# Placing a side stream of weight tiles in a two-block network kernel: where its loads, dots and transposes stand

## The chip, the cores and the metric

One core of a Trainium2 chip runs the whole program in one launch. The metric is device time in microseconds (us). The engines are TensorE (PE, with its weight loads shown apart as PEld), VectorE (DVE), ScalarE (ACT), GpSimd (POOL) and SyncE (SP), which issues nearly all transfers.

## What is computed

256 tokens of width 1024 go through two blocks. The first block has two layers; each has a SwiGLU feed-forward, a token mixer (convolution, state space, attention) and a second feed-forward. Ahead of each of these, and in its residual sum, stand shifts, scales and gates that come from a vector `c` through a large matrix `ada_w`:

```python
for l in range(DEPTH):
    mod = (jax.nn.silu(c) @ ada_w[l] + ada_b[l]).reshape(bsz, 3, 3, 1, D_MODEL)
    u = modulate(h, mod[:, 0, 0], mod[:, 0, 1])            # h * (1 + scale) + shift
    y = swiglu_ffn(u, ffn_w_gate[l, 0], ffn_w_up[l, 0], ffn_w_down[l, 0])
    h = layer_norm(DN_ALPHA * h + MACARON_WEIGHT * mod[:, 0, 2] * y, ln_g[l, 0], ln_b[l, 0])
    u = modulate(h, mod[:, 1, 0], mod[:, 1, 1])
    y = hybrid_token_mixer(u, ...)
    h = layer_norm(DN_ALPHA * h + mod[:, 1, 2] * y, ln_g[l, 1], ln_b[l, 1])
    u = modulate(h, mod[:, 2, 0], mod[:, 2, 1])
    y = swiglu_ffn(u, ffn_w_gate[l, 1], ffn_w_up[l, 1], ffn_w_down[l, 1])
    h = layer_norm(DN_ALPHA * h + MACARON_WEIGHT * mod[:, 2, 2] * y, ln_g[l, 2], ln_b[l, 2])
```

The second block (two more layers with a mixer and a feed-forward) takes no such values.

## The kernel before

**Sections and units.** The program is a list of sections that follow each other: FFN00, mixer0, FFN01 (layer 0), FFN10, mixer1, FFN11 (layer 1), then the second block. A section is a list of units. A unit is half a weight chunk: one transfer of 128 x 1024 f32 (512 KB) on SP into a ring of 4 buffers (`load_half`, L179), a split into a rounded high part on ACT (`hi`, L185) and a rest on DVE (`lo`, L186), and some 12 to 24 matmuls that use both (L282 to L284, L295 to L297). `run` traces the splits up to four units ahead of the matmuls. Between units, `step_sides` moves side work on at a given rate per unit: convolutions (`ca`, L1203), attention, state space, and the modulation stream.

**The modulation stream** (`ada_stream`). There are 18 columns (2 layers x 9) of 8 tiles each. A tile is one transfer of 512 KB (L489, ring of 3 buffers, `ada`) and one dot on DVE that multiplies it with `crow` and sums along the row (L490). The first 16 tiles are done by `First.start`; 128 are left for the stream. After the eighth tile of a column a bias is added (L503). Each third column (a gate) is also turned into a row: a PE transpose (L508), an ACT copy and a small store to `growd`, from which the closing norm of a section fetches it (`Ln.fetch`). `need` runs the stream on by force when a section wants values that are not there yet. `set_pace` sets the stream's rate: 26 tiles for each FFN and each mixer, spread over most of its units; `Ln.affine`, near a section's end, sets it to zero.

**What sets the order.** A scheduler of the tile framework orders the traced instructions of each engine, by its own estimates, within what dependencies allow. `behind(ins)` puts an edge without a semaphore: instructions traced inside it stand behind `ins` on that engine. An engine then runs its list strictly in order, and so does SP with its transfers: an instruction that waits holds all behind it.

**The close of a section.** `Ln.stats` (L606, L607) and `norm_T` (L430 and on) make the next section's operand from the accumulators `y`; PE has little else to do there.

Of the kernel before, what the change touches and what calls it, by code (L numbers as in the profile page):

```python
# [11 lines left out]
F32 = mybir.dt.float32  # L12
# [3 lines left out]
ALU = mybir.AluOpType  # L16
# [3 lines left out]
P = 128  # L20
T = 256
D = 1024
KT = 8
DEPTH = 2
# [81 lines left out]
def net_kernel(ctx, tc, a, out, dbg=None):  # L106
    nc = tc.nc
    V, S, G, E = nc.vector, nc.scalar, nc.gpsimd, nc.tensor

    const = ctx.enter_context(tc.tile_pool(name="const", bufs=1))  # L110
# [17 lines left out]
    def tp_tile():  # L128
        return p_tp.tile([P, 512], F32, tag="tp", name="tp")

    def rt(tag, n, bufs, dt=F32):
        return ring.tile([P, n], dt, tag=tag, name=tag, bufs=bufs)
# [4 lines left out]
    def f(ap):  # L137
        return ap.bitcast(F32)
# [13 lines left out]
    adb = const.tile([P, DEPTH, 72], F32, name="adb")  # L152
# [22 lines left out]
    def load_half(src, half, raw=None):  # L175
        n = max(D, src.shape[-1] // 2)
        if raw is None:
            raw = wraw.tile([P, DW], F32, tag="raw", name="raw")[:, :n]
        state["load"] = nc.sync.dma_start(raw, src[:, half * n:(half + 1) * n])  # L179
        return raw  # L180

    def split_half(src, half, c, room=None, eng=V):
        raw = load_half(src, half)
        hi, lo = room() if room else (wsp.tile([P, DW], F32R, tag=t, name=t)[:, :raw.shape[-1]] for t in ("hi", "lo"))
        S.activation(hi, raw, AF.Copy)  # L185
        eng.tensor_tensor(lo, raw, f(hi), op=ALU.subtract)  # L186
        return tuple(x.rearrange("p (k c) -> p k c", c=c) for x in (hi, lo))

    def split(u):
        u.w = split_half(u.ch.src, u.half, u.c, u.early or u.room)  # L190
# [6 lines left out]
    def set_early(items):  # L197
        units = [it for it in items if isinstance(it, Unit)][:4]
        for i, u in enumerate(units):
            u.early = lambda i=i: spare(i)  # L200
        return units
# [9 lines left out]
    def add_side(gen, rate, front=True):  # L211
        sides.insert(0 if front else len(sides), [gen, rate, 0.0])
        return gen
# [17 lines left out]
    state = {"live": 0}  # L231
# [17 lines left out]
    def behind(ins):  # L249

        es = ExitStack()
        for i in ins:
            es.enter_context(tc.issue_after(i.ins))
        return es
# [214 lines left out]
    mods, pcols = {}, {}  # L469
# [3 lines left out]
    def load_pcol(l):  # L473
        t = big.tile([P, NPC], F32, tag="pcol", name="pcol")
        late_load(t, a["pcol"][l])
        pcols[l] = t
# [7 lines left out]
            E.matmul(tp, ones[0:1, :P], crow[0:1, hs], start=True, stop=True)  # L484
            S.activation(crow[:, hs], tp, AF.Silu)

    def ada_tile(l, j, k, col, raw):
        n = D
        nc.sync.dma_start(raw, a["adaw"][l, j, k // 2][:, (k % 2) * n:(k % 2 + 1) * n])  # L489
        V.scalar_tensor_tensor(raw, raw, 1.0, crow, op0=ALU.mult, op1=ALU.mult, accum_out=col[:, k:k + 1])  # L490


    pace = {"after": ()}

    def ada_stream():
        for l, j in [(l, j) for l in range(DEPTH) for j in range(9)][2:]:
            col = const.tile([P, KT], F32, name="mod%d_%d" % (l, j))
            for k in range(KT):
                with behind(pace["after"]):
                    ada_tile(l, j, k, col, rt("ada", D, 3))  # L500
                pace["after"] = ()
                yield
            V.tensor_add(col, col, adb[:, l, j * 8:j * 8 + 8])  # L503
            mods[(l, j)] = col
            if j % 3 == 2:
                yield
                tp = tp_tile()
                E.transpose(tp[0:KT, :P], col, ident)  # L508
                gr = rt("t1", T, 4)[0:KT, :P]
                S.activation(gr, tp[0:KT, :P], AF.Copy, scale=(1.0 if j == 5 else 0.5))  # L510
                S.dma_start(growd[l * 3 + j // 3].rearrange("(k p) -> k p", p=P), gr)
                mods[(l, j, "row")] = True

    def set_pace(r, after=None):

        if "gen" not in pace:
            pace["gen"] = add_side(ada_stream(), 0.0, front=False)
        for s in sides:
            if s[0] is pace["gen"]:
                s[1] = r  # L520
        if after is not None:
            pace["after"] = after
# [236 lines left out]
    def ffn(cols, down, nj, src, act, rows, nxt):  # L759

        xT = lambda: src.xT
        y, hids, items = {}, {}, []

        def hidden(j):
            st = []

            def evac(ps):
                r = act(st, ps)
                if r is not None:
                    hids[j] = split_hidden(r)  # L770
            its = []
            for c in cols(j):
                its += proj_cols(c, xT, evac)
            return its
        hold = {"nx": nxt(y)}
        n0 = NFIRST if isinstance(src, First) else 2 // len(cols(0))
        done = 0
        for j in range(n0 - 1, nj):
            if j >= n0:
                items += hidden(j)  # L780
            elif isinstance(src, First):
                first = sum((cols(i) for i in range(n0)), [])
                items.append(lambda: src.start(first, rows, hids))
                continue
            else:
                items += first_hidden(sum((cols(i) for i in range(n0)), []), xT, rows, lambda: None, hids)
            if j == n0 + 1:
                items.append(src.residual)
            items += sum(down_items(y, hids, down, nj, range(done, j), hold), [])
            done = j  # L790
            per = 2 * len(cols(0)) + 2
            if j == nj - 1 - 32 // per:
                items.append(lambda: start_fetch(hold["nx"], 0.2))
            if j == nj - 1 - 24 // per:
                items.append(lambda: early(hold["nx"], 4, 0.25))
            if j == nj - 1:
                items.append(lambda: hold["nx"].prefetch())
        items += sum(down_items(y, hids, down, nj, [nj - 1], hold), [])
        return items, hold["nx"]
# [1072 lines left out]
    def ffn_section(cols, down, nj, act, rows, nxt, tiles):  # L1872
        src = cur
        items, nx = ffn(cols, down, nj, src, act, rows, nxt)
        src.pre += set_early(items)
        us = [i for i, it in enumerate(items) if isinstance(it, Unit)]
        rate = tiles / (len(us) - 18)
        if isinstance(src, First):
            items.insert(us[1], lambda: set_pace(rate, src.ins))
            items.insert(us[1], lambda: src.finish())  # L1880
        elif rate:
            items.insert(us[3], lambda: set_pace(rate, src.ins))
        return items, nx

    def mixer_section(fn, l, nxt, tiles=0.0):
        items, nx = fn(l, cur, nxt)
        src = cur
        src.pre += set_early(items)
        if tiles:
            units = [i for i, it in enumerate(items) if isinstance(it, Unit)]  # L1890
            rate = tiles / (len(units) - 16)
            items.insert(units[8], lambda: set_pace(rate, src.ins))
        return items, nx

    def close(nx):

        def start():
            nx.operand(0)
            state["after"] = nx.ins
            nx.operand(1)  # L1900
        return [lambda: nx.stats(1)] + ([start] if hasattr(nx, "operand") else [])

    for l in range(DEPTH):
        if l:
            prog.append(lambda l=l: load_pcol(l))
        for i in range(3):
            nxt = lambda y, l=l, i=i, src=cur: Ln(l, i, y, src)
            if i == 1:
                its, nx = mixer_section(mixer1, l, nxt, 26.0)
            else:  # L1910
                n = i // 2
                its, nx = ffn_section(lambda j: [a["wg"][l, n, j], a["wu"][l, n, j]], a["wd"][l, n], DFF // T, swiglu,
                                      swiglu_rows, nxt, 26.0)
            prog += its
            if not nx.last:
                prog += close(nx)
            cur = nx
# [56 lines left out]
    for l in range(DEPTH):  # L1974
# [5 lines left out]
        its, nx = mixer_section(mixer2, l, lambda y, l=l: Rms(y, lambda: qcols[l][:, QC_NF:QC_NF + 8]))  # L1980
        prog += its + close(nx)
        cur = nx
        if l + 1 < DEPTH:
            nxt = lambda y, l=l, src=cur: Rms(y, lambda: qcols[l + 1][:, QC_NM:QC_NM + 8], src)
        else:
            nxt = lambda y, src=cur: Out(y, src)
        its, nx = ffn_section(lambda j: [a["ff1"][l, j]], a["ff2"][l], DFF2 // T, relu2, lambda ps: relu2(None, ps), nxt, 0.0)
# [196 lines left out]
```

## Time and profile before

| | |
|---|---|
| median of three runs | 2521.87 us (2512.83 to 2522.38) |
| profiled execution | 2518.11 us |
| its span | 2516.3 us |
| mean granted TensorE clock | 0.987 of full speed |
| busy: PE / PEld / DVE / ACT | 95% / 87% / 73% / 54% |
| moved | 490 MB, mean 195 GB/s |

PE is busy nearly all the time, so what can be moved lies in the stretches where it is not, and in those where it is busy at the lower clock: a granted clock of 0.5 is 1.2 GHz, 1.0 is 2.4 GHz, and the same matmuls then count as more busy time. The sections are of few kinds, so the same code can be compared with and without the stream beside it. The section boundaries used below (213, 706, 926, 1122, 1582 and 1774 us) stand in the closes, within a few us of the first row of the next section's operand.

### The profile page before, as it was taken

The page shows a single profiled execution, that of the slowest core. Times are in us where ns is not written, and L with a number is a line of the kernel's source. Part 1 is how long each engine was busy: PE and PEld are TensorE (multiplying, and loading weights), DVE is VectorE, ACT ScalarE, POOL GpSimd, SP SyncE. Part 2 cuts the span into 40 slices and gives each one's busy share as a digit, 9 for nine tenths or more (in the row PEclk, how much of TensorE's full clock was granted, in tenths as well). Part 3 has the DMA queues.
Part 4 walks back from the last instruction along what each step waited for, and adds up shares of the span by engine and source line. Part 5 has one row for each costly group of instructions (what it writes and reads, how often), then busy time and mean ns, then how long its engine had stood idle before and what let it go on. Part 6 is the DMA issues. An engine that isn't in the chain of part 4 may idle for free. (4 is left out here: it accounts for less than half of the span.)

```text
span 2516.3 us, 42234 instructions
## 1 busy us (share of the span) xinstructions
PE 2401.0 (95%) x16444; PEld 2186.2 (87%) x16444; DVE 1838.0 (73%) x3262; ACT 1360.7 (54%) x2392; POOL 70.1 (3%) x128
## 2 busy tenths in 40 slices
PE   8999999999899979999999999999899999999999
PEld 6997889889789869988899898899789898799898
DVE  7789988899787677568988996655766555666544
ACT  5445677644544434455676555545465555565554
POOL 0000000000000000000000000000100000100000
PEclk9999999999999989999999999999999999999999
DMA  9897533356878867655433456467346566436464
GB/s 333 305 363 270 195 128 97 120 166 219 285 240 295 298 218 238 218 176 187 162 102 91 130 181 226 143 194 236 126 134 192 156 187 222 142 110 226 150 185 142
DMA packets 140058, 490.00 MB, mean 195 GB/s; under 512 B 16249, under 2 KB 21969, under 8 KB 139858
## 3 DMA queue, kind: packets, MB, share of 16 engines
q1 hardware_dynamic: 132194, 476.61, 57.3%
q10 hardware_dynamic: 7664, 10.69, 1.3%
q8 instruction: 129, 2.11, 0.3%
q14 instruction: 71, 0.58, 0.1%
HBM read 481.94 MB, written 5.31 MB: 194 GB/s over the span
## 5 line engine op out<-in xcount | busy, mean ns | idle before, releaser
L185 ACT ACTIVATE hi<-raw 128x1024 fp32r<-128x1024 f32 (+1 forms) x676 | 713.4, 1059 | 706.9 <-PE mm L283 386.4
L186 DVE TENSOR_TENSOR lo<-raw,hi 128x1024 fp32r<-128x1024 f32 (+1 forms) x676 | 825.0, 1223 | 313.5 <-ACT hi L185 311.4
L282 PE MATMUL mm<-xTh,hi 128*128 128x256 f32 x2896 | 826.8, 286 | 11.3 <-ACT seg L915 4.2
L284 PE MATMUL mm<-xTh,lo 128*128 128x256 f32 x2896 | 821.7, 284 | 3.9 <-DVE lo L186 3.9
L283 PE MATMUL mm<-xTl,hi 128*128 128x256 f32 x2896 | 821.7, 284 | 2.2 <-DVE xTl L453 2.2
L282 PEld LDWEIGHTS mm<-xTh,hi 128*128 128x128 f32 x2896 | 550.7, 190 | 16.7 <-ACT seg L915 4.3
L283 PEld LDWEIGHTS mm<-xTl,hi 128*128 128x128 f32 x2896 | 550.4, 190 | 6.5 <-DVE xTl L453 3.0
L284 PEld LDWEIGHTS mm<-xTh,lo 128*128 128x128 f32 x2896 | 550.3, 190 | 5.6 <-DVE lo L186 5.1
L297 PE MATMUL y<-hi,q 128*128 128x512 f32 x664 | 263.0, 397 | 0.3 <-DVE q L700 0.3
L296 PE MATMUL y<-lo,q 128*128 128x512 f32 x552 | 219.0, 397 | 6.6 <-DVE lo L186 6.5
L295 PE MATMUL y<-hi,q 128*128 128x512 f32 x552 | 219.5, 399 | 5.3 <-ACT q L699 5.2
L490 DVE SCALAR_TENSOR_TENSOR ada<-ada,crow 128x1024 f32<-128x1024 f32 x128 | 156.2, 1223 | 73.9 <-DMA ada<-in_adaw_dram 73.5
L1203 DVE SCALAR_TENSOR_TENSOR ca<-av,pcol,ca 128x226 f32<-128x226 f32 (+25 forms) x480 | 209.0, 468 | 0.3
L297 PEld LDWEIGHTS y<-hi,q 128*128 128x128 f32 x664 | 125.7, 189 | 31.1 <-DVE q L700 0.9
L296 PEld LDWEIGHTS y<-lo,q 128*128 128x128 f32 x552 | 104.0, 189 | 31.9 <-DVE lo L186 10.4
L295 PEld LDWEIGHTS y<-hi,q 128*128 128x128 f32 x552 | 104.0, 189 | 29.0 <-ACT q L699 7.2
L295 PE MATMUL y<-hi,xTh 128*128 128x512 f32 (+1 forms) x288 | 113.5, 394 | 2.8 <-DVE e8b L829 1.5
L283 PE MATMUL mm<-xyl,hi 128*128 128x256 f32 x384 | 109.9, 287 | 5.1 <-DVE xyl L413 5.1
L282 PE MATMUL mm<-xyh,hi 128*128 128x256 f32 x384 | 109.9, 287 | 3.3 <-ACT t2d L1371 3.0
L284 PE MATMUL mm<-xyh,lo 128*128 128x256 f32 x384 | 109.8, 286 | 3.1 <-DVE lo L186 3.1
L297 PE MATMUL y<-hi,xTl 128*128 128x512 f32 (+1 forms) x288 | 111.6, 388 | 0.0
L296 PE MATMUL y<-lo,xTh 128*128 128x512 f32 (+1 forms) x288 | 111.0, 385 | 0.0
(480 smaller groups left out, 3688.0 us busy)
## 6 DMA issues: line engine op xcount, KB each, us to landing
ada<-in_adaw_dram SPq DMA_DIRECT2D x128, 512.0 KB, 5.9
raw<-in_ff_dram SPq DMA_DIRECT2D x128, 512.0 KB, 4.5
raw<-in_wg_dram SPq DMA_DIRECT2D x88, 512.0 KB, 5.1
raw<-in_wu_dram SPq DMA_DIRECT2D x88, 512.0 KB, 4.7
raw<-in_wd_dram SPq DMA_DIRECT2D x88, 512.0 KB, 4.7
raw<-in_wG_dram SPq DMA_DIRECT2D x48, 512.0 KB, 3.8
raw<-in_wkv_dram SPq DMA_DIRECT2D x16, 512.0 KB, 4.4
raw<-in_wval_dram SPq DMA_DIRECT2D x16, 512.0 KB, 3.9
```

The costliest lines, as they stand in the source:

```text
L185: S.activation(hi, raw, AF.Copy)
L186: eng.tensor_tensor(lo, raw, f(hi), op=ALU.subtract)
L282: E.matmul(ps, wh[:, wk + k], xh, start=(k == 0), stop=False)
L283: E.matmul(ps, wh[:, wk + k], xl, start=False, stop=False)
L284: E.matmul(ps, wl[:, wk + k], xh, start=False, stop=(k == nk - 1))
L295: return [E.matmul(ps, xh, wh[:, kk, cs], start=first, stop=False), E.matmul(ps, xh, wl[:, kk, cs], start=False, stop=False), E.matmul(ps, ...
L296: E.matmul(ps, xh, wl[:, kk, cs], start=False, stop=False),
L297: E.matmul(ps, xl, wh[:, kk, cs], start=False, stop=last)]
L490: V.scalar_tensor_tensor(raw, raw, 1.0, crow, op0=ALU.mult, op1=ALU.mult, accum_out=col[:, k:k + 1])
L1203: V.scalar_tensor_tensor(ca[:, k, s:T], av[:, 0:T - s], caw[:, k, w:w + 1], ca[:, k, s:T], op0=ALU.mult, op1=ALU.add)
```

## The change

The load and the dot of a tile become separate functions. The stream is written as steps. Step n traces the load of tile n, placed behind the newest weight load on SP; then, if one is due, the transpose of a gate's column that was completed three steps before; then the dot of tile n-1, placed behind the newest `lo` on DVE. So a dot is traced one step later than its load. No tile, transpose or bias is added or dropped.

The rates change too: FFN00 38 tiles, FFN01 31, FFN10 31, FFN11 16 (all spread over 9 units more than before), and 11 in each mixer, between its 30th and 62nd unit alone, after which the rate is zero.

```diff
-        eng.tensor_tensor(lo, raw, f(hi), op=ALU.subtract)
+        state["lo"] = eng.tensor_tensor(lo, raw, f(hi), op=ALU.subtract)
...
     def ada_stream():
-        for l, j in [(l, j) for l in range(DEPTH) for j in range(9)][2:]:
-            col = const.tile([P, KT], F32, name="mod%d_%d" % (l, j))
-            for k in range(KT):
-                with behind(pace["after"]):
-                    ada_tile(l, j, k, col, rt("ada", D, 3))
-                pace["after"] = ()
-                yield
-            V.tensor_add(col, col, adb[:, l, j * 8:j * 8 + 8])
-            mods[(l, j)] = col
-            if j % 3 == 2:
-                yield
+        todo = [(l, j, k) for l in range(DEPTH) for j in range(9) for k in range(KT)][2 * KT:]
+        cols, raws, turn = {}, {}, []
+        for n in range(len(todo) + 4):
+            if n < len(todo):
+                raws[n] = rt("ada", D, 3)
+                with behind([state["load"]]):
+                    ada_load(*todo[n], raws[n])
+            if turn and n >= turn[0][0]:
+                _, l, j, col = turn.pop(0)
                 tp = tp_tile()
                 E.transpose(tp[0:KT, :P], col, ident)
...
+            if 0 < n <= len(todo):
+                l, j, k = todo[n - 1]
...
+                with behind([state["lo"], *pace["after"]]):
+                    ada_dot(k, col, raws.pop(n - 1))
+                pace["after"] = ()
+                if k == KT - 1:
+                    V.tensor_add(col, col, adb[:, l, j * 8:j * 8 + 8])
+                    mods[(l, j)] = col
+                    if j % 3 == 2:
+                        turn.append((n + 3, l, j, col))
+            yield
...
-        rate = tiles / (len(us) - 18)
+        rate = tiles / (len(us) - 9)
...
-            rate = tiles / (len(units) - 16)
-            items.insert(units[8], lambda: set_pace(rate, src.ins))
+            items.insert(units[29], lambda: set_pace(tiles / 32, src.ins))
+            items.insert(units[61] + 1, lambda: set_pace(0.0))
...
-                its, nx = mixer_section(mixer1, l, nxt, 26.0)
+                its, nx = mixer_section(mixer1, l, nxt, 11.0)
...
-                                      swiglu_rows, nxt, 26.0)
+                                      swiglu_rows, nxt, ((38.0, 31.0), (31.0, 16.0))[l][n])
```

Counted in the instruction order from one section's close to the next, the dots stand as follows. Before: FFN00 34, its close 2, mixer0 33, its close 4, FFN01 38, its close 5, FFN10 11, mixer1 1. After: FFN00 40, mixer0 11, FFN01 32, FFN10 32, mixer1 11, FFN11 2, and none in a close. The order of the second block is the same in both.

First place: SP's list in the middle of FFN01 (`wg`, `wu`, `wd` are its weights, `adaw` the stream's tiles). Before:

```order
L179 DMA raw<-in_wg_dram 128x1024
L489 DMA ada<-in_adaw_dram 128x1024
L179 DMA raw<-in_wu_dram 128x1024 x2
L489 DMA ada<-in_adaw_dram 128x1024
L179 DMA raw<-in_wd_dram 128x1024
L489 DMA ada<-in_adaw_dram 128x1024
L179 DMA raw<-in_wd_dram 128x1024
L489 DMA ada<-in_adaw_dram 128x1024
L179 DMA raw<-in_wg_dram 128x1024
L489 DMA ada<-in_adaw_dram 128x1024
```

After:

```order
L489 DMA ada<-in_adaw_dram 128x1024
L179 DMA raw<-in_wu_dram 128x1024 x2
L489 DMA ada<-in_adaw_dram 128x1024
L179 DMA raw<-in_wd_dram 128x1024 x2
L489 DMA ada<-in_adaw_dram 128x1024
L179 DMA raw<-in_wg_dram 128x1024 x2
L489 DMA ada<-in_adaw_dram 128x1024
```

Two weight halves now stand between two tiles, where before there was mostly one.

Second place: DVE's list at the close of mixer0 (`y` the accumulator, `row` the residual, `xTl` the operand's rest, `mod` the columns). Before:

```order
L606 TENSOR_TENSOR y_7486<-y_7486,grow 128x512
L606 TENSOR_TENSOR row_7217<-row_7217,y_7486 128x512
L490 SCALAR_TENSOR_TENSOR ada,mod_1_8090<-ada,crow 128x1024
L607 BN_STATS bnst<-row_7217 128x6
L606 TENSOR_TENSOR y_7486<-y_7486,grow 128x512
L490 SCALAR_TENSOR_TENSOR ada,mod_1_8090<-ada,crow 128x1024
L606 TENSOR_TENSOR row_7217<-row_7217,y_7486 128x512
L453 TENSOR_TENSOR xTl<-t_7657,xTh 128x2x128
```

After:

```order
L626 TENSOR_TENSOR y_7457<-y_7457,grow 128x512
L626 TENSOR_TENSOR row_7194<-row_7194,y_7457 128x512
L627 BN_STATS bnst<-row_7194 128x6
L626 TENSOR_TENSOR y_7457<-y_7457,grow 128x512
L626 TENSOR_TENSOR row_7194<-row_7194,y_7457 128x512
L627 BN_STATS bnst<-row_7194 128x6
L453 TENSOR_TENSOR xTl<-t_7625,xTh 128x2x128
```

The two dots between the steps of the close are gone from it.

Third place: DVE's list in the middle of mixer1, where attention (`amx`, `aneg`, `cf`), state space (`seg`) and convolution (`ca`) run side by side. Before:

```order
L1335 TENSOR_TENSOR row_12820<-row_12820,tp 128x64
L1222 SCALAR_TENSOR_TENSOR av<-av,mm 128x512
L413 TENSOR_TENSOR xyl<-tp,xyh 128x2x128
L951 TENSOR_REDUCE amx<-y_13701 128x4
L1203 SCALAR_TENSOR_TENSOR ca<-av,pcol,ca 128x245
L954 TENSOR_SCALAR aneg<-amx 128x4
L186 TENSOR_TENSOR lo<-raw,hi 128x1024
L1203 SCALAR_TENSOR_TENSOR ca<-av,pcol,ca 128x246
```

After:

```order
L971 TENSOR_REDUCE amx<-y_13668 128x4
L413 TENSOR_TENSOR xyl<-tp,xyh 128x2x128
L974 TENSOR_SCALAR aneg<-amx 128x4
L1223 SCALAR_TENSOR_TENSOR ca<-av,pcol,ca 128x245
L492 SCALAR_TENSOR_TENSOR ada,mod_7_11457<-ada,crow 128x1024
L1223 SCALAR_TENSOR_TENSOR ca<-av,pcol,ca 128x246
L528 TENSOR_TENSOR mod_7_11457<-mod_7_11457,adb 128x8
L186 TENSOR_TENSOR lo<-raw,hi 128x1024
```

A dot of the stream stands here now, ahead of the next `lo`, in a place that had none.

## Rows read from the trace of the kernel before

**Rows 1.** Engine busy times by section: stretch; length, PE, PEld, DVE, ACT, POOL; clock, DMA share, GB/s.

```profile
0.00:213.00 213.00, 199.24 (x1170) 172.75 (x1170) 169.29 (x241) 99.19 (x124) 0.76 (x5) 1.00 0.92 331
213.00:706.00 493.00, 456.82 (x3264) 420.92 (x3264) 432.48 (x927) 289.52 (x597) 19.19 (x40) 0.97 0.55 180
706.00:926.00 220.00, 199.02 (x1342) 181.42 (x1340) 161.26 (x227) 92.91 (x118) 1.19 (x2) 0.97 0.80 274
926.00:1122.00 196.00, 194.19 (x1341) 180.31 (x1341) 127.18 (x161) 91.39 (x116) 2.17 (x2) 0.98 0.65 215
1122.00:1582.00 460.00, 441.51 (x3262) 408.01 (x3262) 392.78 (x851) 286.61 (x593) 18.90 (x40) 1.00 0.47 152
1582.00:1774.00 192.00, 189.99 (x1336) 176.86 (x1336) 113.03 (x128) 90.71 (x114) 0.90 (x2) 1.00 0.58 190
```

**Rows 2.** Dots alone (L490, two records each) by section: length, DVE busy, clock, DMA.

```profile
213.00:706.00 493.00, 44.21 (x72) 0.97 0.55 180
706.00:926.00 220.00, 55.62 (x91) 0.97 0.80 274
926.00:1122.00 196.00, 14.47 (x24) 0.98 0.65 215
1122.00:1582.00 460.00, 1.23 (x2) 1.00 0.47 152
```

**Rows 3.** Both mixers cut at the same places of their work, columns as rows 1.

```profile
213.00:345.00 132.00, 121.46 (x791) 109.36 (x791) 122.43 (x246) 81.61 (x152) 2.70 (x7) 0.97 0.61 206
345.00:451.00 106.00, 103.99 (x813) 96.24 (x813) 89.35 (x263) 82.52 (x226) 6.87 (x19) 1.00 0.32 98
451.00:706.00 255.00, 231.37 (x1664) 215.32 (x1662) 220.70 (x420) 125.39 (x220) 9.63 (x14) 0.95 0.61 201
1122.00:1248.00 126.00, 118.75 (x796) 107.09 (x797) 113.73 (x231) 81.55 (x153) 2.65 (x7) 1.00 0.52 171
1248.00:1350.00 102.00, 101.48 (x801) 94.64 (x801) 86.49 (x258) 80.28 (x223) 8.06 (x19) 1.00 0.31 94
1350.00:1582.00 232.00, 221.28 (x1670) 206.28 (x1668) 192.55 (x364) 124.77 (x219) 8.19 (x14) 1.00 0.51 167
```

**Rows 4.** Dots alone in three stretches of mixer0, columns as rows 2.

```profile
213.00:345.00 132.00, 12.25 (x20) 0.97 0.61 206
345.00:451.00 106.00, 1.22 (x2) 1.00 0.32 98
451.00:706.00 255.00, 30.74 (x50) 0.95 0.61 201
```

**Rows 5.** Inner parts of three FFN sections, columns as rows 1.

```profile
60.00:200.00 140.00, 139.99 (x940) 128.22 (x938) 111.93 (x152) 65.59 (x82) 0.00 (x0) 1.00 0.94 334
720.00:900.00 180.00, 169.73 (x1188) 157.16 (x1187) 131.05 (x169) 75.21 (x84) 0.00 (x0) 0.99 0.82 286
948.00:1110.00 162.00, 162.00 (x1155) 152.23 (x1154) 98.45 (x108) 75.42 (x84) 0.00 (x0) 1.00 0.70 234
```

**Rows 6.** Tile ada, 720 to 900: idle of DVE before it (us, times); then a dot's duration.

```profile
L490 DVE SCALAR_TENSOR_TENSOR ada<-ada,crow x38: 1214/1225/1228, 719.5 to 898.1; 128x1024 f32<-128x1024 f32 x38
...
  DMA ada<-in_adaw_dram: 43.4, 25
```

**Rows 7.** DVE timeline in FFN01: start, us, operation [idle before <-what ended it].

```profile
802.71 2.36 DVE L186 TENSOR_TENSOR lo<-raw,hi 128x1024 fp32r<-128x1024 f32 x2
806.71 1.23 DVE L490 SCALAR_TENSOR_TENSOR ada<-ada,crow 128x1024 f32<-128x1024 f32 x1 [1.65 <-DMA ada<-in_adaw_dram]
...
807.86 1.22 DVE L186 TENSOR_TENSOR lo<-raw,hi 128x1024 fp32r<-128x1024 f32 x1
```

**Rows 8.** SP's queue: what its transfers waited for, us in total, times, longest.

```profile
SPq L489 <- DVE ada L490: 139.3, 46, 11.2
```

**Rows 9.** A PE gap in mixer0, timeline of PE, columns as rows 7.

```profile
330.32 0.55 PE L282 MATMUL mm<-xTh,hi 128*128 128x256 f32 x1 [4.16 <-ACT seg L915]
```

**Rows 10.** The 4 us in which that gap ends, columns as rows 1.

```profile
328.00:332.00 4.00, 1.68 (x8) 1.71 (x9) 4.00 (x8) 4.00 (x10) 0.00 (x0) 0.77 0.31 97
```

More of the change, by code (lines that the diff above doesn't have):

```diff
@@ L485, in silu_c, with ada_load, ada_dot, ada_tile @@
             S.activation(crow[:, hs], tp, AF.Silu)
-    def ada_tile(l, j, k, col, raw):
+    def ada_load(l, j, k, raw):
         n = D
         nc.sync.dma_start(raw, a["adaw"][l, j, k // 2][:, (k % 2) * n:(k % 2 + 1) * n])
+    def ada_dot(k, col, raw):
         V.scalar_tensor_tensor(raw, raw, 1.0, crow, op0=ALU.mult, op1=ALU.mult, accum_out=col[:, k:k + 1])
+    def ada_tile(l, j, k, col, raw):
+        ada_load(l, j, k, raw)
+        ada_dot(k, col, raw)
     pace = {"after": ()}
     def ada_stream():
-        for l, j in [(l, j) for l in range(DEPTH) for j in range(9)][2:]:
-            col = const.tile([P, KT], F32, name="mod%d_%d" % (l, j))
-            for k in range(KT):
-                with behind(pace["after"]):
-                    ada_tile(l, j, k, col, rt("ada", D, 3))
-                pace["after"] = ()
-                yield
-            V.tensor_add(col, col, adb[:, l, j * 8:j * 8 + 8])
-            mods[(l, j)] = col
-            if j % 3 == 2:
-                yield
+        todo = [(l, j, k) for l in range(DEPTH) for j in range(9) for k in range(KT)][2 * KT:]
[7 more added lines that the diff above has]
+                _, l, j, col = turn.pop(0)
                 tp = tp_tile()
@@ L512, in ada_stream @@
                 mods[(l, j, "row")] = True
+            if 0 < n <= len(todo):
+                l, j, k = todo[n - 1]
+                if k == 0:
+                    cols[l, j] = const.tile([P, KT], F32, name="mod%d_%d" % (l, j))
+                col = cols[l, j]
+                with behind([state["lo"], *pace["after"]]):
[7 more added lines that the diff above has]
+            yield
     def set_pace(r, after=None):
```

## The prediction

> **What bounds the kernel now.** I read the granted clock first, then busy times by section, then the dots of the modulation stream alone in the same sections, and last the waits of DVE, SP and PE inside the sections that stood out. PE is the bound: over the four sections from 926 on it is busy nearly always [rows 1]. What the reader should see is that equal code runs at unequal speed. Mixer0 and mixer1 are the same program with other weights, and so are FFN01, FFN10 and FFN11. Mixer0 takes 493 us and mixer1 460; FFN01 takes 220 us, FFN10 196 and FFN11 192 [rows 1]. What differs is the stream: a dot leaves two records, so mixer0 has 36 tiles, FFN01 45 or 46, FFN10 12, mixer1 one [rows 2], and FFN11 none. Mixer0's 33 us more are 17.7 us more of idle PE (36.2 against 18.5) and 15.3 us more of busy PE at the same count of matmuls, with a mean clock of 0.97 against 1.00 [rows 1]. FFN01's 28 us more are 19 us of idle and 9 us of busy time, again at 0.97. So a stall is paid twice here: as a gap, and as matmuls at the lower level behind it. One gap of 4.16 us [rows 9] has a granted clock of 0.77 in the 4 us in which it ends [rows 10].
>
> Where the stream hurts differs. In the mixers it takes DVE's time. Cut at equal places of the work, mixer0 is 6, 4 and 23 us longer than mixer1 in three stretches [rows 3], with 10, 1 and 25 tiles [rows 4]. In the first DVE is busy 122 of 132 us, in the last 221 of 255; in the middle of mixer1 it has 15.5 of 102 us free [rows 3]. In the FFNs DVE has time enough (131 of 180 us) but PE still idles 10 us there [rows 5]: a dot stands in DVE's list before its tile has landed, DVE idles 43.4 us on 25 such waits [rows 6], and the `lo` behind it, which PE needs, is late [rows 7].
>
> **The change part by part.** No instruction is added or dropped: 128 transfers, 128 dots of 1.22 us [rows 6], 6 transposes, 16 biases. The edges are between instructions of one engine and carry no semaphore. All of it is a question of place, so I price a section by its tiles.
>
> *Mixers.* One early tile cost 6 us / 9 tiles (mixer1 has one of its own) = 0.67 us, one late tile 23 / 25 = 0.92 us [rows 3, 4]. The middle's 4 us came with a DVE that was 2.9 us busier, 1.2 of it the dot [rows 3, 4]; I take them as work pushed back from the early stretch, not as the price of one tile. In the new order each mixer has 2 dots in the early stretch, 6 in the middle and 3 in the late one. The middle's price is not in the trace, since hardly a dot stood there: it lies between 0 (the 15.5 us free) and 1.22 us (every dot on the path). Six dots bring DVE to 86.5 + 7.3 = 94 of 102 us, 92%, which is nearest to the early stretch at 93%, so I take 0.67. A mixer without tiles takes 460 - 0.7 = 459.3 us; with 11 tiles 459.3 + 2 x 0.67 + 6 x 0.67 + 3 x 0.92 = 467.4. **Mixer0: -25.6. Mixer1: +7.4.** With the middle at its ends a mixer takes 463.4 to 470.7. The dots that stood in mixer0's close go with this.
>
> *FFN01 and FFN10.* A tile's price lies between 0 and 28 us / 45 = 0.62 us (FFN01 against FFN11). Zero is what FFN00 shows: 32 tiles between 60 and 200 with PE busy 139.99 of 140 us; and FFN10 from 948 to 1110, PE busy 162 of 162 [rows 5]. The new order attacks just the wait that makes the 0.62: the dot is traced a step later than its load, about two units at this rate, and stands behind the newest `lo`, so its tile should have landed. DVE has the room for 32 dots: FFN11's 113 us and 39 us of dots make 152 of 192. I take 0.2, nearer to the two rows at zero: 192 + 32 x 0.2 = 198.4 us each. **FFN01: -21.6. FFN10: +2.4.** FFN10's own 4 us over FFN11 lie ahead of 948 and hang on the close before it, which had 5 dots. At the ends: -28 and -4, or -8 and +16.
>
> *FFN00* goes from 34 tiles, and 2 in its close, to 40, and its PE cannot get faster [rows 5]. Its transfers are the question: 334 GB/s at a DMA share of 0.94 [rows 5] make 355 GB/s at a share of 1, and 6 more tiles are 3.1 MB, 8.8 us of it; the free 6% of 140 us are 8.4 us. So 0 to 8.8, and I take **+4**: the room is there on average, but not everywhere. The Trainium skill ("Perfetto Trace Analysis", Roofline) says that a core whose neighbour rests can pull more than its share of 358 GB/s, up to the some 435 GB/s of its 16 DMA engines. By that rule there is room for the tiles at no cost and the sum would be 4 us lower; no mean over a long stretch here shows more than 334, so I go by the row.
>
> *FFN11* gets 2 tiles: +0.4. *The transposes* three steps later: they are 6, off the path of PE but for short waits, and the rows are needed only late in a section; nothing. *The second block* has the same order: nothing.
>
> Sum: -25.6 + 7.4 - 21.6 + 2.4 + 4 + 0.4 = -33.0. The profiled execution took 2518.1 us (span 2516.3), so 2485.1. It lies 3.8 us under the median of the three runs, inside their spread; I forecast **2485**.
>
> **The rivals.**
>
> *B: the FFN price stays.* A load placed behind the newest weight load also stands ahead of all later ones. It waits for its ring buffer, that is for the dot of three tiles before, and SP holds the weights behind it. Before, SP waited 139.3 us in 46 cases for this [rows 8]. Dots now come later, which frees the buffers later. Against it: the split runs four units ahead, so a weight can be late by some units before PE sees it, and at two units a tile the dot three tiles back is old. If each tile still costs 0.62 in FFN01, FFN10 and FFN11 and FFN00 pays its 8.8: -18.2 - 8.2 + 15.8 + 1.2 + 8.8 = -0.6, that is 2517. No change.
>
> *C: the mixers' middle breaks (slower).* The attention and state-space steps there are short and hang on each other across ACT, DVE and PE; the dots now stand among them, twelve in the two mixers, and a dot ahead of a `lo` or of a step that PE waits for opens a gap. A gap of that kind is on record in mixer0's early stretch, where PE waits 4.16 us for a step of the state space [rows 9]; it costs some 0.23 x 4 = 0.9 us more in clock [rows 10]. If every middle dot did that: -33.0 - 12 x 0.67 + 12 x 5.1 = +20, that is 2538. Slower by over 0.5% begins at 4.5 us a dot. For it: mixer1's middle was at 101.5 of 102 us, so everything there can only lose. Against it: the single dot of mixer0's middle left PE busy 104 of 106 us [rows 3].
>
> *F: everything placed is free.* All prices zero but the mixers' early and late tiles: -29.6 + 3.4 - 28 - 4 = -58 us, that is 2460.
>
> **How the numbers follow.** Forecast (2462 to 2508): 0.70. F: 0.09. B: 0.13. C: 0.08. Half a per cent, about what a measurement of this kernel can tell from no change, is 12.6 us. Faster takes the forecast and F, 0.79; B is the same, 0.13; C is slower, 0.08. The range goes from F's 2460 to B's 2518, which leaves out C and what of F lies lower.
>
> **What would show it.** Right: mixer0 near 467 us with a clock near 1.00; FFN01 and FFN10 near 198 us each; DVE's waits for stream tiles in FFN01 well under 43 us; no dots in the closes. FFN00 longer by a few us, with a DMA share near 1. Wrong: `lo` of FFN01 still late behind dots, or `hi` on ACT waiting for weights (B); PE gaps in the middle of either mixer, with a lower clock behind them (C); FFN00 longer by 10 us or more.

## The result and the profile after

The changed kernel takes 2537.84 us (median of 4 runs, 2532.56 to 2541.09) against 2521.52 for the kernel before in the same session (2512.83 to 2522.38): a ratio of 1.0069, 95% interval 1.0055 to 1.0084. It is slower by 0.7%, and 53 us above the forecast. The profiled execution took 2532.56 us, its span is 2530.4 us, its mean granted clock 0.982 (2516.3 us and 0.987 before).

By section, from busy times of the changed kernel (columns as in [rows 1]; the last line is the whole second block):

```profile
0.00:232.00 232.00, 206.81 (x1177) 176.61 (x1178) 180.17 (x259) 102.86 (x132) 0.76 (x5) 0.98 0.89 316
232.00:707.00 475.00, 448.93 (x3259) 414.27 (x3258) 403.82 (x872) 285.94 (x589) 16.63 (x40) 0.98 0.49 161
707.00:907.00 200.00, 193.68 (x1347) 179.24 (x1348) 149.66 (x201) 94.16 (x122) 1.12 (x2) 0.99 0.80 267
907.00:1106.00 199.00, 195.00 (x1343) 180.79 (x1343) 150.19 (x202) 93.32 (x119) 1.10 (x2) 0.98 0.77 262
1106.00:1592.00 486.00, 456.57 (x3259) 421.68 (x3258) 404.10 (x871) 286.68 (x589) 18.42 (x40) 0.96 0.48 157
1592.00:1789.00 197.00, 192.49 (x1339) 179.12 (x1338) 119.17 (x142) 90.66 (x116) 2.02 (x3) 0.99 0.58 188
1789.00:2530.00 741.00, 723.71 (x4729) 648.69 (x4728) 436.43 (x721) 409.12 (x732) 25.91 (x36) 0.99 0.53 164
```

FFN01 gave what was forecast. But FFN00 is 15 us longer, mixer1 27 us, and mixer0, with a third of its former dots, only 16 us shorter. Mixer1, before at a clock of 1.00 [rows 1], now runs at 0.96.

The table sets all kernels of this study side by side: length of each section in us (to the end of its last statistics instruction on DVE, line L627, L607 before, L628 in e11) and, behind the slash, its dots (half of their records; FFN00's hold the 16 that are no part of the stream).

| kernel | FFN00 | mixer0 | FFN01 | FFN10 | mixer1 | FFN11 | 2nd block |
|---|---|---|---|---|---|---|---|
| before | 216.8/51 | 492.1/36 | 221.2/45 | 194.6/11 | 459.7/1 | 195.5/0 | 736.4 |
| changed | 231.8/56 | 475.7/11 | 199.8/32 | 198.3/32 | 486.8/11 | 196.8/2 | 741.2 |
| e1 mixer1 empty | 232.5/56 | 476.8/11 | 194.6/39 | 194.8/38 | 460.2/0 | 196.0/0 | 741.1 |
| e2 fourth buffer | 223.7/56 | 476.6/11 | 197.1/32 | 200.1/32 | 485.2/11 | 196.0/2 | 743.5 |
| e3 no pins | 223.3/57 | 479.4/27 | 215.9/45 | 194.4/13 | 461.2/1 | 195.9/1 | 739.2 |
| e4 old rates | 225.0/51 | 491.6/27 | 198.7/32 | 198.2/32 | 464.5/2 | 196.4/0 | 739.6 |
| e6 free in FFN00 | 222.4/56 | 483.9/11 | 195.4/39 | 195.3/38 | 464.8/0 | 196.0/0 | 740.8 |
| e7 free to mixer0 | 222.5/57 | 468.0/10 | 195.3/39 | 194.6/38 | 465.5/0 | 195.9/0 | 741.7 |
| e8 more in mixer0 | 222.3/47 | 479.9/19 | 195.3/38 | 194.9/39 | 464.0/0 | 195.5/1 | 737.8 |
| e9 early window | 217.7/56 | 470.5/11 | 195.0/39 | 194.2/38 | 458.5/0 | 196.4/0 | 739.4 |
| e10 small dots | 234.1/56 | 479.7/11 | 201.1/32 | 201.4/32 | 461.3/11 | 196.0/2 | 738.4 |
| e11 no lag in FFN00 | 217.2/56 | 471.3/11 | 194.9/39 | 194.6/38 | 462.2/0 | 194.9/0 | 745.7 |
| e12 load pin alone | 218.9/57 | 475.4/12 | 207.2/38 | 197.8/37 | 462.0/0 | 197.6/0 | 742.3 |
| e13 dot pin alone | 220.4/56 | 467.4/11 | 195.9/39 | 194.2/38 | 462.0/0 | 196.1/0 | 736.4 |

Each line is one execution. The second block has the same order everywhere and still spreads over 736 to 746 us, empty mixers over 458.5 to 465.5, and mixer0 over 475.7 to 483.9 in five kernels whose DVE lists are the same there (changed, e1, e2, e6, e10). A difference of 5 us in one section is thus no evidence by itself, nor 8 us in a mixer. The changed kernel's 4.8 us more in the second block are of that kind.

### The profile page after: what moved, and what is told of

It reads as the page before. It is cut to its first block, busy times and chain, and to the rows that moved or that the text cites. A ratio compares the mean times of both kernels' runs of the same rounds, so it can differ in the third digit from the quotient of the medians.

```text
span 2530.4 us, 42246 instructions
## 1 busy us (share of the span) xinstructions
PE 2417.2 (96%) x16444; PEld 2200.4 (87%) x16444; DVE 1843.5 (73%) x3262; ACT 1362.7 (54%) x2392; POOL 66.0 (3%) x128
## 5 line engine op out<-in xcount | busy, mean ns | idle before, releaser
L282 PEld LDWEIGHTS mm<-xTh,hi 128*128 128x128 f32 x2896 | 556.5, 192 | 25.7 <-ACT seg L934 9.2
L1223 DVE SCALAR_TENSOR_TENSOR ca<-av,pcol,ca 128x244 f32<-128x244 f32 (+20 forms) x480 | 207.7, 463 | 0.5
```

The costliest lines, as they stand in the source:

```text
L282: E.matmul(ps, wh[:, wk + k], xh, start=(k == 0), stop=False)
L1223: V.scalar_tensor_tensor(ca[:, k, s:T], av[:, 0:T - s], caw[:, k, w:w + 1], ca[:, k, s:T], op0=ALU.mult, op1=ALU.add)
```

## The experiments

### Mixer1: an emptied section, and small dots in the same places

Two runs ask where mixer1's 27 us come from. The first takes its eleven tiles away:

```diff
-                its, nx = mixer_section(mixer1, l, nxt, 11.0)
+                its, nx = mixer_section(mixer1, l, nxt, (11.0, 0.0)[l])
-  ... ((38.0, 31.0), (31.0, 16.0))[l][n])
+  ... ((38.0, 37.0), (37.0, 16.0))[l][n])
```

> The changed kernel with no tile of the modulation stream planned in the second layer's mixer; its eleven tiles go to FFN01 and FFN10 (37 each instead of 31). Theory D (each dot that lies among the mixer's short instructions costs a gap and clock behind it): mixer1 goes from 487 to about 460 us, FFN01 and FFN10 gain 1 to 2 us each, the kernel comes to 2513 us (2508 to 2518). Theory R (the scheduler's new order of the mixer's own instructions, whatever dots lie in it, costs the 27 us): mixer1 stays over 478 us and the kernel over 2529.

Measured: mixer1 460.2 us, the kernel 2498.19 us, ratio to before 0.9918 (0.9890 to 0.9946). Theory D holds for mixer1. The kernel gained more than I expected, mostly since FFN01 and FFN10, with 6 to 7 dots more each, did not get longer but 4 to 5 us shorter.

Mixer1 cut at equal places of its work, first the changed kernel, then with mixer1 empty:

```profile
1106.00:1201.00 95.00, 92.74 (x586) 82.72 (x584) 82.45 (x166) 58.22 (x107) 1.39 (x3) 0.99 0.53 178
1201.00:1404.00 203.00, 186.11 (x1344) 170.34 (x1344) 167.01 (x449) 131.77 (x339) 13.96 (x32) 0.94 0.37 120
1404.00:1592.00 188.00, 177.72 (x1329) 168.62 (x1330) 154.64 (x257) 96.70 (x145) 3.07 (x5) 0.98 0.56 185
```

```profile
1099.00:1194.00 95.00, 91.73 (x583) 81.27 (x582) 82.89 (x167) 58.37 (x108) 1.39 (x3) 1.00 0.50 173
1194.00:1372.00 178.00, 174.05 (x1344) 160.83 (x1343) 155.39 (x428) 130.33 (x338) 13.64 (x32) 1.00 0.33 107
1372.00:1559.00 187.00, 177.09 (x1331) 167.75 (x1332) 153.83 (x254) 97.07 (x145) 3.08 (x5) 0.98 0.55 183
```

All but 1 or 2 us is in the stretch that holds the eleven dots: 203 against 178 us for the same 1344 matmuls. PE's idle time there is 16.9 us against 4.0, and its busy time 186.1 against 174.1 at a clock of 0.94 against 1.00. A dot costs 25 / 11 = 2.3 us, half as gap and half as clock, though it is 1.2 us long and DVE has 36 of the 203 us free. Of PE's waits there, two for `sac`, a convolution tap of the state space, make 7.1 us, and waits for steps of attention 8.4.

The longest gap, in DVE's timeline of the changed kernel (start, length, operation, idle before it):

```profile
1206.23 1.21 DVE L492 SCALAR_TENSOR_TENSOR ada<-ada,crow 128x1024 f32<-128x1024 f32 x1
...
1207.75 1.21 DVE L186 TENSOR_TENSOR lo<-raw,hi 128x1024 fp32r<-128x1024 f32 x1
...
1210.41 1.22 DVE L186 TENSOR_TENSOR lo<-raw,hi 128x1024 fp32r<-128x1024 f32 x1
1211.55 0.47 DVE L1302 SCALAR_TENSOR_TENSOR sac<-mm,pcol,sac 128x255 f32<-128x255 f32 x1
1213.24 0.79 DVE L879 TENSOR_TENSOR stk<-e,stk 128x128 fp32r<-128x128 f32 x2 [1.22 <-ACT stk L877]
...
1215.30 1.21 DVE L186 TENSOR_TENSOR lo<-raw,hi 128x1024 fp32r<-128x1024 f32 x1
1216.43 0.47 DVE L1302 SCALAR_TENSOR_TENSOR sac<-mm,pcol,sac 128x253 f32<-128x253 f32 x1
...
1217.19 1.64 DVE L1302 SCALAR_TENSOR_TENSOR sac<-mm,pcol,sac 128x254 f32<-128x254 f32 x4
```

The `sac` taps read the matmul buffer that PE needs next. Ahead of them DVE has a dot, three `lo` and a wait of 1.22 us for ACT. Here is PE's next matmul, and then busy times (columns as in [rows 1]) of 10 us behind the gap:

```profile
1218.59 0.55 PE L282 MATMUL mm<-xTh,hi 128*128 128x256 f32 x1 [4.21 <-DVE sac L1302]
```

```profile
1219.00:1229.00 10.00, 10.00 (x65) 9.82 (x65) 7.41 (x14) 4.90 (x9) 0.00 (x0) 0.74 0.36 121
```

PE waits 4.21 us, and then works 10 us without a pause at a mean clock of 0.74, that is about half of the time at the lower level (1.2 GHz). With mixer1 empty the same gap is 1.50 us, and what ends it is ACT:

```profile
1208.36 0.36 PE L282 MATMUL mm<-xTh,hi 128*128 128x256 f32 x1 [1.50 <-ACT sac L1299]
```

The scheduler had also set mixer1's own instructions in another order, so that the dots might be innocent. The second run keeps every load, pin and tile, and makes only the dots from the 116th tile on short (the rest of their columns is left out):

```diff
-    def ada_dot(k, col, raw):
-        V.scalar_tensor_tensor(raw, raw, 1.0, crow, ...)
+    def ada_dot(k, col, raw, w=D):
+        V.scalar_tensor_tensor(raw[:, :w], raw[:, :w], 1.0, crow[:, :w], ...)
-                    ada_dot(k, col, raws.pop(n - 1))
+                    ada_dot(k, col, raws.pop(n - 1), P if n > 115 else D)
```

> The changed kernel with the dots of the tiles from the 116th on, mixer1's eleven and the two behind them, over 128 of their 1024 columns only (the rest of these dots is left out; loads, pins and order stay). Theory T (VectorE's time for the dot, ahead of work that frees a matmul buffer, makes the gaps): with dots of about 0.2 us instead of 1.2, mixer1 goes from 487 to 462 to 468 and the gap of 4.2 us there to under 2.5. Theory O (the order and the waits that come with the pinned dots cost it, whatever their length): mixer1 stays over 478.

Measured: mixer1 461.3 us with its eleven dots, now 0.27 us long; the kernel 2514.18 us, one run. The same stretch reads:

```profile
1211.00:1389.00 178.00, 170.93 (x1309) 157.94 (x1310) 151.52 (x435) 126.27 (x325) 13.75 (x32) 0.99 0.41 133
```

178 us, as without dots. (The cut falls 35 matmuls earlier here; the whole section, 461.3 against 460.2 us, says the same.) Theory O falls as it was put: pins, transfers and the number of dots are the same, SP's list is the same instruction by instruction, and they cost nothing. What mixer1 pays for is the length of the dots in that place: eleven times 0.94 us taken from DVE gave back 25 us.

Theory T is not shown in full, because the order did not stay. Up to just behind the first short dot DVE's list is that of the changed kernel; from there to the end of mixer1 the scheduler set it otherwise in some 80 places. The gap of 4.21 us is 2.38 here:

```profile
1223.69 0.29 DVE L879 TENSOR_TENSOR stk<-e,stk 128x128 fp32r<-128x128 f32 x1 [0.95 <-ACT stk L877]
...
1224.57 0.47 DVE L1302 SCALAR_TENSOR_TENSOR sac<-mm,pcol,sac 128x253 f32<-128x253 f32 x1
...
1225.73 1.21 DVE L186 TENSOR_TENSOR lo<-raw,hi 128x1024 fp32r<-128x1024 f32 x1
1227.48 0.36 PE L282 MATMUL mm<-xTh,hi 128*128 128x256 f32 x1 [2.38 <-DVE sac L1302]
```

From the dot's start to the first `stk` behind the wait for ACT it is 7.0 us with the long dot and 6.7 with the short one, so that wait hides nearly all of the dot. From there to PE's matmul it is 5.4 against 3.8 us, and no dot stands ahead of the taps: the changed kernel has `lo` ahead of the next taps, e10 has taps ahead of `lo`. In this gap the order thus did more than the dot's own time. How the 25 us divide between the time of a long dot and the order that the scheduler makes around it, no run shows.

### FFN00: what holds SP's queue

One run gives the first 30 tiles a fourth buffer; two others lack both pins, or keep them at the old rates.

```diff
-                raws[n] = rt("ada", D, 3)
+                raws[n] = bt("e8b", 2 * D)[:, :D] if n < 30 and n % 4 == 3 else rt("ada", D, 3)
```

> The changed kernel with a fourth buffer for the first 30 tiles of the stream (every fourth of them lies in a buffer that FFN00 does not use otherwise). Theory Q (with the pins the SP queue stands behind a stream load that waits for a dot to free its buffer, and the weight loads behind it land late): the SP queue's waits for the dots in FFN00 shrink from 99 us to under 40, FFN00 goes from 231.8 to 220 to 225 us, the span from 2530 to 2519 to 2525. Theory S (the pins cost something else, or the DMA engines have no room for more): FFN00 stays within 2 us of 231.8.

Measured, one run: span 2522.0 us, FFN00 223.7, that is 8.1 us shorter at the same 56 dots. (With the buffer for the first 38 tiles, as first planned, the program deadlocks, so there is no time for it.) Theory Q has the time right, but its count was wrong: SP's waits for dots were 66.5 us in 33 cases, not 99 us (I had added the cases to the microseconds). They fell by less than it said. Below are 60 to 200 us (columns as [rows 5]) and SP's waits for dots between 60 and 222 us (us in total, times, longest). These waits in the kernel before:

```profile
SPq L489 <- DVE ada L490: 15.7, 8, 7.1
```

The changed kernel:

```profile
60.00:200.00 140.00, 132.27 (x843) 117.88 (x842) 107.59 (x149) 58.70 (x74) 0.00 (x0) 0.99 0.92 321
```

```profile
SPq L489 <- DVE ada L492: 66.5, 33, 4.2
```

With the fourth buffer:

```profile
60.00:200.00 140.00, 136.43 (x900) 122.84 (x899) 113.71 (x157) 62.83 (x78) 0.00 (x0) 1.00 0.95 345
```

```profile
SPq L489 <- DVE ada L492: 45.1, 23, 4.6
```

More bytes per second go through, 345 against 321 GB/s, so the DMA engines had room; SP's queue stood. A stream load that waits for a dot three tiles back holds the weight loads behind it, and PE, busy 139.99 of 140 us before [rows 5], is busy 132.27. Theory S falls.

```diff
-                with behind([state["load"]]):
+                with behind([]):
...
-                with behind([state["lo"], *pace["after"]]):
+                with behind(pace["after"]):
```

> The changed kernel without its two pins (the loads not behind the newest weight load, the dots not behind the newest lo part); the new placement, the lag and the late transposes stay. If the pins hold the stream's buffers too long, FFN00 comes down to 218 to 224 us; if the pinned dots break the mixers, mixer1 comes down from 487 to 465 to 472. If the new placement alone is at fault, both stay within 4 us of what they are (231, 487) and the kernel within 5 us of 2538. If the pins are what brought FFN01 and the others down, FFN01 goes from 200 to over 210.

Measured: 2513.76 us, ratio 0.9987 (0.9975 to 0.9999). FFN00 223.3 us with 57 dots, FFN01 back at 215.9: the pins cost 8.5 us in the one section and earn 16 in the other (there with 32 dots against 45). In all, FFN00 takes 231.8 to 234.1 us in the three kernels with both pins and this rate, and 217.2 to 223.3 in the eight without pins there. Mixer1's 461.2 us say nothing on the pins, since without them the stream was all but done when it came (one dot).

```diff
-        rate = tiles / (len(us) - 9)
+        rate = tiles / (len(us) - 18)
...
-            items.insert(units[29], lambda: set_pace(tiles / 32, src.ins))
-            items.insert(units[61] + 1, lambda: set_pace(0.0))
+            rate = tiles / (len(units) - 16)
+            items.insert(units[8], lambda: set_pace(rate, src.ins))
...  (and 26.0 tiles for every section)
```

> The changed kernel with the old placement (26 tiles planned per section, the old windows and denominators); the pins, the dots one step later and the late transposes stay. If these three are free by themselves, the sections read as in the kernel before (216, 492, 221, 195, 460, 195) and the kernel 2517 to 2527 us. If the hold on the stream's buffers is what costs, at 26 tiles too, FFN00 is over 221 and the kernel over 2530. If they are what makes the mixers break, mixer0 is over 500 us.

Measured: 2515.13 us, ratio 0.9995 (0.9981 to 1.0008). FFN00 is 225.0 us with the same 51 dots that take 216.8 in the kernel before, over 221 as the hold would have it, but the kernel is 15 us under the 2530 that I had put beside it. SP's waits for dots are there at the old rate too, 64.5 us in 30 cases. What they cost is less sure: 225.0 lies 2 to 8 us over the executions without pins, and the five dots more of the changed kernel take a pinned FFN00 7 us further. So it is the pins, and with pins the tiles count. Mixer0 takes 491.6 us with 27 dots, as long as before with 36; mixer1 had two dots and says nothing. FFN01 has its gain of 22 us here without the new rates (198.7 us, 32 dots).

Then the pins are left off for the first tiles only, on top of the empty mixer1:

```diff
-                with behind([state["load"]]):
+                with behind([state["load"]] if n >= 40 else []):
...
-                with behind([state["lo"], *pace["after"]]):
+                with behind([*([state["lo"]] if n > 40 else []), *pace["after"]]):
```

> The run with mixer1 empty, and the two pins left off for the first 40 tiles of the stream, those of FFN00. If the pins' hold in FFN00 is the 8.5 us by which the run without pins was shorter there (223.3 against 231.8), FFN00 is 222 to 225 us and the span 2485 to 2490. If the run without pins was shorter because the scheduler was free elsewhere too, FFN00 stays over 228.

Measured, one run: span 2498.5 us, FFN00 222.4 as expected, but the span was 8.5 to 13.5 us over: mixer0, by the same DVE list, took 483.9 us instead of 476.8, and the empty mixer1 464.8 instead of 460.2.

One kernel, built on e7 below, took the lag of one step from FFN00's dots as well:

```diff
-            if 0 < n <= len(todo):
-                l, j, k = todo[n - 1]
+            m = n if n < 40 else n - 1
+            if n != 40 and m < len(todo):
+                l, j, k = todo[m]
```

> The run with the pins left off in FFN00 and mixer0, the dots of the first 40 tiles in the same step as their load again, not one step later. FFN00 was 216.8 us in the kernel before and 222 to 223 without pins, with 47 dots as with 57. If the lag is what is left, FFN00 is 216 to 219 and the kernel 4 to 6 us faster than the run before it (2474 to 2476 us); if the number of tiles or their window is, FFN00 stays at 221 to 224 and the kernel within 3 us of 2480.

Measured: 2478.48 us, ratio 0.9832 (0.9810 to 0.9853). FFN00 217.2 us, but the kernel is not measurably faster than e7 (0.9818), where I had expected 4 to 6 us. And FFN00 took 217.7 us in e9, with the lag, 56 dots and the very DVE and PE lists by which it took 222.4 in e6. Between 60 and 200 us e9 moved 354 GB/s, e6 341:

```profile
60.00:200.00 140.00, 139.15 (x931) 127.23 (x930) 117.43 (x163) 64.62 (x80) 0.00 (x0) 1.00 0.96 354
```

```profile
60.00:200.00 140.00, 136.60 (x895) 123.97 (x894) 114.05 (x159) 63.09 (x79) 0.00 (x0) 0.99 0.94 341
```

So what is left over 216.8 us, 0.4 to 6.5 us, differs from one execution to the next, and neither lag nor tiles are shown to cause it.

### Mixer0: the pin, or the place

```diff
-  ... if n >= 40 ...   ... if n > 40 ...
+  ... if n >= 51 ...   ... if n > 51 ...
```

> As the run before it, with the pins left off for the first 51 tiles, those of FFN00 and mixer0. Theory P (the pinned dot is what makes a dot in the mixer's middle cost 1.5 to 2.4 us): mixer0 with its 11 tiles goes from 476 to 460 to 468, the kernel to 2476 to 2484 us. Theory W (a dot costs that in the mixer's middle, pinned or not): mixer0 stays at 472 to 480, the kernel at 2484 to 2492.

Measured: 2479.77 us, ratio 0.9818 (0.9779 to 0.9857); mixer0 468.0 us, the end of theory P's range. The dots alone (columns as [rows 2]) show why P is still not proven; e6 first, then e7, each cut at the same places of mixer0's work:

```profile
222.00:317.00 95.00, 0.00 (x0) 1.00 0.54 178
317.00:512.00 195.00, 10.97 (x18) 0.93 0.38 120
512.00:706.00 194.00, 2.46 (x4) 0.99 0.58 188
```

```profile
222.00:317.00 95.00, 9.81 (x16) 1.00 0.63 212
317.00:497.00 180.00, 1.22 (x2) 0.99 0.35 107
497.00:691.00 194.00, 1.22 (x2) 0.97 0.57 186
```

Freed, the dots moved: eight went to the first 95 us, which hold the same work with or without them, within 5 of 585 matmuls. The middle fell from 195 us with nine dots to 180 with one (by the very list of e6 it took 189 us in the changed kernel). Pin and place had changed together; the next run keeps the pins and moves only the planned window, on top of e6:

```diff
-            items.insert(units[29], lambda: set_pace(tiles / 32, src.ins))
-            items.insert(units[61] + 1, lambda: set_pace(0.0))
+            items.insert(units[2], lambda: set_pace(tiles / 32, src.ins))
+            items.insert(units[34] + 1, lambda: set_pace(0.0))
```

> The run with the pins left off in FFN00 alone, mixer0's eleven tiles, pinned as there, planned from its 3rd to its 35th unit instead of from its 30th to its 62nd. Theory W (what a dot costs hangs on the stretch it lies in; the pin only holds it there): the dots lie between 5 and 180 us of mixer0, the five that remain past 100 us cost 1.5 to 2.4 us each, and mixer0 goes from 483.9 to 468 to 476. Theory P (a pinned dot costs 1.5 to 2.4 us wherever it stands): mixer0 stays at 478 to 486.

Measured: 2473.61 us, one run; mixer0 470.5 us. Its dots by the same cuts:

```profile
218.00:313.00 95.00, 9.82 (x16) 1.00 0.63 211
313.00:499.00 186.00, 3.66 (x6) 0.97 0.33 106
499.00:688.00 189.00, 0.00 (x0) 0.99 0.57 190
```

Pinned dots in the first stretch are free as well; the three past it cost the middle 186 - 180 = 6 us against the one of e7, while the late stretch, without a dot, is 5 us shorter. In e13 below, with the same window and the dots pinned, mixer0 is 467.4 us. Theory W: the place costs, and the pin only holds the dots there.

> As the run before it, with 27 tiles planned in FFN00 instead of 38 and 22 in mixer0's window instead of 11. The run without pins had 27 dots in mixer0 at 479.4 us, and a tile more in FFN00 cost 1.1 to 1.4 us (six more, 6.5 to 6.8 us longer). If both hold here, FFN00 comes to 212 to 217, mixer0 to 478 to 484, and the kernel is 3 to 8 us faster than the run before it. If a dot in mixer0's middle costs 1.5 us each, pinned or not, mixer0 is over 488 and the kernel 2 to 8 us slower than the run before it.

(e7 with rates of 27 in FFN00 and 22 in mixer0.) Measured: 2495.31 us, ratio 0.9892 (0.9862 to 0.9922), 15.5 us slower than e7. Neither reading held. Mixer0 came to 479.9 us with nine dots more, as the first had it, but FFN00 stayed at 222.3 us with ten dots fewer: I had taken FFN00's 6.5 us over the kernel before for a price per tile, and there is none to see between 47 and 57 dots. Nothing was gained to set against mixer0.

### FFN01: which of the two pins

Both kernels are e9 with one of its pins taken off:

```diff
 e12:
-                with behind([*([state["lo"]] if n > 40 else []), *pace["after"]]):
+                with behind(pace["after"]):
 e13:
-                with behind([state["load"]] if n >= 40 else []):
+                with behind([]):
```

> The run with mixer0's early window, with the pin on the dots taken off everywhere; from the 41st tile on the loads stay behind the newest weight load. Without both pins FFN01 took 215.9 us (45 dots), with both 194.6 to 195.4 (39 dots). Theory L (what helped the FFNs is that a stream load no longer goes ahead of a weight load on SP's queue): FFN01 and FFN10 stay at 194 to 199 us and the kernel at 2470 to 2480. Theory D (it is that a dot no longer stands ahead of a lo part on VectorE, waiting for its tile): FFN01 goes over 208 and the kernel over 2485.

> The run with mixer0's early window, with the pin on the loads taken off everywhere; from the 41st tile on the dots stay behind the newest lo part. Theory L: FFN01 goes over 208 us and the kernel over 2485. Theory D: FFN01 and FFN10 stay at 194 to 199 and the kernel at 2470 to 2480. If both pins are needed, each of the two runs has FFN01 at 200 to 208.

Measured: e12 2496.69 us, ratio 0.9901 (0.9875 to 0.9927), FFN01 207.2; e13 2475.44 us, ratio 0.9833 (0.9811 to 0.9855), FFN01 195.9 and FFN10 194.2. What ended DVE's idle time (us, times, longest) between 700 and 900 us, most of FFN01 in each of them (705 to 905 in e3), in e3 without pins, e12, e13 and the changed kernel:

```profile
DVE ada L492 <- DMA ada<-in_adaw_dram: 43.1, 28, 4.0
```

```profile
DVE ada L492 <- DMA ada<-in_adaw_dram: 35.2, 23, 3.8
```

```profile
DVE lo L186 <- ACT hi L185: 32.7, 37, 3.8
```

```profile
DVE lo L186 <- ACT hi L185: 30.7, 35, 1.7
```

With the load pin alone DVE still stands 35.2 us before tiles that have not landed, with `lo` behind the dot, and PE waits for `lo`:

```profile
PE mm L284 <- DVE lo L186: 7.9, 9, 2.0
```

With the dot pin, alone or not, that wait is gone; what DVE waits for is now `hi`, and PE does not notice. Theory D holds, though FFN01 is 0.8 us short of the 208 that it named for e12; the load pin adds nothing in FFN01 (195.9 us without it, 195.0 with it in e9). In FFN10 the dot pin is worth only 3.6 us (197.8 against 194.2). Which of the two pins holds SP in FFN00 was not taken apart.

## Why the prediction was wrong, step by step

From the forecast's -33.0 to the measured +14.1 us of span there are 47.1 us: mixer1 19.7, FFN00 11.0, mixer0 9.2, the second block 4.8, and 2.4 in the three other FFNs.

- **The bound and the double price of a stall: right.** PE is the bound, and a gap is paid again in clock. The 0.9 us that I took for the clock behind a 4 us gap [rows 10] were too little: 10 us at 0.74 behind the gap of 4.21 us are 2.6 us.
- **The price of a middle dot: wrong, and the step that failed.** The count was right: by the cuts of [rows 3] mixer1 has 2, 6 and 3 dots. The price was read from the wrong quantity. I took DVE's share of busy time, 92% after the change, found it like the early stretch and took 0.67 us, at most 1.22, "every dot on the path". In its place the runs showed 2.3 us a dot, almost twice the dot's length: 12.9 us of gaps and, behind them, 12.1 us of matmuls at the lower clock (e1), nearly all of it gone when the dots were short (e10). The bound from above left out the very clock that the first part of the prediction had shown. How a long dot makes its gaps, by its own time or by the order that the scheduler sets around it, stays open. By the cuts of [rows 3] mixer1 now reads:

```profile
1102.00:1234.00 132.00, 123.66 (x808) 111.91 (x807) 114.22 (x229) 82.14 (x155) 2.71 (x7) 0.96 0.53 177
1234.00:1352.00 118.00, 109.58 (x799) 101.28 (x798) 94.39 (x272) 82.76 (x224) 7.40 (x19) 0.93 0.32 102
1352.00:1589.00 237.00, 224.21 (x1659) 209.08 (x1658) 196.41 (x374) 122.61 (x213) 8.31 (x14) 0.98 0.52 171
```

DVE's 94 us of busy time were forecast to the microsecond; the stretch is 118 us, where 102 + 4 were forecast, so that DVE's share is 80% and not 92%. The early and late stretches are 6 and 5 us longer, against a forecast of 1.3 and 2.8. What the trace of before did show was the row at 1.00: a stretch in which PE idles 0.5 of 102 us has no room that a busy share could measure.
- **An early dot at 0.67 us: too dear.** Eight dots in the first 95 us of mixer0 cost nothing that the cuts can show (e7, e9). The early stretch of the prediction is 132 us long and reaches past them; what made it 6 us longer in mixer0 of the kernel before, no run shows.
- **FFN01 and FFN10: right in size and mechanism.** -21.4 and +3.7 against -21.6 and +2.4. The dot behind the newest `lo` is what did it (e13). The price of 0.2 us a tile was not needed: 39 and 38 dots take 194.6 and 194.8 us (e1), as FFN11 with none. That FFN11 took 192 us was a matter of the cut, since by the table's it takes 195.5; so part of the match is luck. What the changed kernel loses to e1, 4 to 5 us, has one PE wait of 4.2 us for ACT in FFN01's end; why it is there with 32 dots and not with 39 is open.
- **FFN00: the wrong resource.** I asked what room the DMA engines had, and the +4 for it stands unproven: FFN00 has reached 217 to 218 us with 56 dots. The cost was rival B's queue, which I had priced in the other FFNs and given to FFN00 as no more than its 8.8. It is 8 us or more (e2, e3, and the spread given there). My argument against it, that the split runs four units ahead and a dot three tiles back is old, does not hold where the stream's rate is highest: the dots are a step later and pinned, and the ring is three. The Trainium skill ("Perfetto Trace Analysis", Roofline) says that a core whose neighbour rests can pull up to some 435 GB/s. The trace goes part of the way, 354 GB/s over 140 us (e9) where I knew 334. By that rule the sum would have been 4 us lower and the miss as much larger.
- **The rivals.** C named the mechanism (a middle dot opens a gap, paid in clock) and had its 2538 us by chance: it took 5.1 us a dot in both mixers, 53 us, where the runs show 2.3 in mixer1 and 1 to 2 in mixer0 (189 and 195 us with nine dots against 180 with one), and the rest came from FFN00. Both rivals were partly true at once; I had let each stand alone, so their sum was in no case.

A kernel that beats both came out of the parts: no tiles in mixer1, mixer0's in its first units, the dots pinned behind `lo` after FFN00 and the loads not (e13, ratio 0.9833); e7 (0.9818), e9 and e11 are as fast within what was measured.

## What to carry to other kernels

Work put on an engine with spare time is priced by the place that it takes in that engine's list, not by the engine's busy share: such dots were free in the first 95 us of a mixer and cost 1 to 2.3 us each a little later. A pin that fixes an order also fixes a place, so pin an instruction only where its place is cheap, and pin the consumer behind the urgent work; pinning the load as well earned nothing here. To tell an instruction's time from the disorder that comes with it, shrink it where it stands, and then compare the lists: a scheduler that goes by estimated times may have set the rest anew, as it did here.

## What was not expected of the hardware

Ten microseconds of matmuls without a pause ran at a granted clock of 0.74 behind a gap of 4.21 us, and in mixer1's middle 12.9 us more of gaps came with 12.1 us more of busy time. And a DMA share of 1 was reached at 383 GB/s for 20 us in FFN00 of e7 (share and GB/s are the last two columns), above the 355 that I had worked out from a mean:

```profile
120.00:140.00 20.00, 20.00 (x147) 18.89 (x146) 18.23 (x25) 8.21 (x10) 0.00 (x0) 1.00 1.02 383
```
